# Transposing attention weights by a product with diag(1/sum), and two heads' values as the weights of one output product

## The chip, the cores and the metric

One core of a Trainium2 chip runs the whole program. The metric is the device time of one execution in microseconds (us). The engines are TensorE (PE; its weight loads are PEld), VectorE (DVE), ScalarE (ACT), GpSimd (POOL) and SyncE (SP); SP's queue issues the large loads from memory one after the other.

## The reference

A trunk of two layers over 256 context tokens and 256 latent tokens, model width 1024. Each layer has a mixer with three head groups (a state-space part S5, multi-head latent attention, an mLSTM), an output projection, and a mixture of 64 experts of which each token takes 8. All products are in fp32. Both parts are modulated by rows `mod = silu(c) @ ada_w + ada_b`. The attention has 8 heads of 64 + 32 columns for queries and keys and 64 columns for values:

```python
def _attend(q_nope, q_rope, k_nope, k_rope, v):
    s = (jnp.einsum('bqhd,bkhd->bhqk', q_nope, k_nope)
         + jnp.einsum('bqhr,bkr->bhqk', q_rope, k_rope))
    p = jax.nn.softmax(s.astype(jnp.float32) * MLA_SCALE, axis=-1).astype(v.dtype)
    return jnp.einsum('bhqk,bkhd->bqhd', p, v)
...
y_lat = jnp.concatenate([s5_lat, mla_lat, ml_lat], axis=-1) @ w_out[layer]
```

Context queries read context alone (256 keys, two blocks of 128), latent queries read context and latent (512 keys, four blocks). The second layer ("last") computes only the 256 latent queries.

## The kernel before, in words

The mixer of a layer has two stages. In the first, the input projections and S5 run; in the second, three Python generators are woven together: `mlstm`, `mla` and `more` (the modulation rows and then the loads of `w_out`). `weave` takes so many steps of each in a round: two of `mlstm`, two of `mla`, one of `more` (a step of `more` is one block of `ada_w`), in an order from the table `PACE` (`Do`); the mLSTM begins six rounds late (`latem`). What a generator issues between two `yield`s stands together in the order of each engine. So if one generator has fewer steps, the others' instructions stand at other places.

`mla` works by items, one head and one segment of queries each (`seg` 1: latent, four key blocks; `seg` 0: context, two; layer 1 has `seg` 1 alone, so 8 items; layer 0 has 16). `scores` (L907) makes two query tiles `s`, the maximum, the exponentials `pr` with their sums, and the reciprocals `sm[:, :, 2:3]`. `turn` (L924) transposes `pr` block by block with `tpose` (L312) into `pt`, key rows on the partitions. `outs` (L933) multiplies: `pt` is the stationary operand, 64 columns of the values `V` the moving one, and each result, 128 queries by 64 columns, is scaled by the reciprocal into `on` (L943 on ScalarE, L945 on VectorE). An item is in three steps of the loop at once: item n scores, n - 1 turns, n - 2 gives its output (three `yield`s an item). At the end four (layer 1: two) further steps transpose `on` (L971 to L976) into `cat`, model columns on the partitions, as the projection needs it.

`more` (L1387) runs the modulation rows: three calls of `ada_pair` in layer 0 and two in layer 1, with eight steps each. A step loads a megabyte `w` (L364) and multiplies it in four column quarters (L366). The last pair of layer 0 copies its sums `ada` on ScalarE (L371) and transposes them (`adac`, L377); the others add the bias on VectorE (L388) and write the rows to memory (L390). Behind the steps come the four megabytes of `w_out` (L353). `w` has four buffers: a load is issued when the step four before it is done. After the streams `post` projects `cat` by `w_out` (`yo`, L1430) for four token tiles (layer 1: two), normalises, and later runs the shared expert, whose weights `sw` (3 MB, L1420) are loaded to a place that the mixer's tiles used.

The order of each engine's instructions is fixed when the program is built. A scheduler puts the loads into SP's order by when their places come free; each engine and each queue then works in that order.

Of the kernel before, what the change touches and what calls it, by code (L numbers as in the profile page):

```python
# [10 lines left out]
F32 = mybir.dt.float32  # L11
BF16 = mybir.dt.bfloat16
I32 = mybir.dt.int32
AF = mybir.ActivationFunctionType
OP = mybir.AluOpType
# [256 lines left out]
class Trunk:  # L272
# [587 lines left out]
    def mla(self, l, qn, kn, kr, mp, cat, last):  # L860
        nc, d, v = self.nc, self.d, self.nc.vector
        n0 = 256 if last else 0
        wq, wkv = self.wq.rearrange("p (a b) -> p a b", a=2), self.wkv[:, :1024]
        kh = [mp.tile([96, NT], F32, name=f"kh{j}") for j in range(4)]
        for j in range(4):
            (v.tensor_copy if j % 2 else nc.scalar.copy)(kh[j][64:96], kr[64:96])
        V = mp.tile([128, 4, 512], F32, name="V")
        on = mp.tile([128, 4, 512], F32, name="on")
        qh = {}

        def values(i):
            ps = self.bank("v")
            nc.tensor.matmul(ps, kn[:, i * 128:(i + 1) * 128], wkv[:, 512:], start=True, stop=True)
            nc.scalar.copy(V[:, i, :], ps)

        def queries(h4):
            pr, pw = self.bank("qr"), self.bank("qw")
            for t, o in ((pr, 512), (pw, 768)):
                for b in range(2):
                    nc.tensor.matmul(t[:, n0:], wq[:, b, o + h4 * 128:o + h4 * 128 + 128], qn[b][:, n0:], start=b == 0, stop=b == 1)  # L880
            t1 = mp.tile([128, 256], F32, name="rp1")
            t2 = mp.tile([128, 256], F32, name="rp2")
            v.tensor_tensor(out=t1, in0=pr[:, 256:], in1=self.c("cos"), op=OP.mult)
            v.tensor_tensor(out=t2, in0=pw[:, 256:], in1=self.c("sin"), op=OP.mult)
            for j in range(4):
                h = 4 * h4 + j
                qh[h] = mp.tile([96, NT], F32, name=f"qh{j}")
                r = slice(32 * j, 32 * j + 32)
                v.tensor_tensor(out=qh[h][64:96, 256:], in0=t1[r], in1=t2[r], op=OP.add)
                if not last:  # L890
                    nc.scalar.copy(qh[h][64:96, 0:256], pr[r, 0:256])
            for p2 in range(2):
                hp = 2 * h4 + p2
                ps = self.bank("qn")
                for b in range(2):
                    nc.tensor.matmul(ps[:, n0:], wq[:, b, hp * 128:hp * 128 + 128], qn[b][:, n0:], start=b == 0, stop=b == 1)
                nc.scalar.copy(qh[2 * hp][0:64, n0:], ps[0:64, n0:])
                v.tensor_copy(qh[2 * hp + 1][0:64, n0:], ps[64:128, n0:])

        def keys(hp):  # L900
            ps = self.bank("kh")
            nc.tensor.matmul(ps, wkv[:, hp * 128:hp * 128 + 128], kn, start=True, stop=True)
            k2 = kh[2 * (hp % 2):2 * (hp % 2) + 2]
            nc.scalar.copy(k2[0][0:64], ps[0:64])
            v.tensor_copy(k2[1][0:64], ps[64:128])

        def scores(it):  # L907
            h, seg = it["h"], it["seg"]
            nk = it["nk"]
            n = nk * 128  # L910
            it["pr"] = pr = mp.tile([128, 2, NT], F32, name="pr", bufs=2)
            it["sm"] = sm = mp.tile([128, 2, 4], F32, name="sm", bufs=4)
            both = self.bank("s") if nk == 2 else None
            for t in range(2):
                qt = seg * 2 + t
                ps = both[:, t * n:(t + 1) * n] if both is not None else self.bank("s")
                nc.tensor.matmul(ps, qh[h][:, qt * 128:(qt + 1) * 128], kh[h % 4][:, :n], start=True, stop=True)
                it[t] = ps
            for t in range(2):
                v.tensor_reduce(out=sm[:, t, 0:1], in_=it[t], axis=AX.X, op=OP.max, negate=True)  # L920
                nc.scalar.activation(pr[:, t, :n], it[t], AF.Exp, bias=sm[:, t, 0:1], accum_out=sm[:, t, 1:2])
            v.reciprocal(sm[:, :, 2:3], sm[:, :, 1:2])

        def turn(it):  # L924
            nk = it["nk"]
            it["pt"] = pt = mp.tile([128, 4, 2, 128], F32, name="pt", bufs=2)
            for t in range(2):
                pp = self.bank("pt")
                for kt in range(nk):
                    self.tpose(pp[:, kt * 128:(kt + 1) * 128], it["pr"][:, t, kt * 128:(kt + 1) * 128])  # L930
                (nc.scalar.copy if t else v.tensor_copy)(pt[:, 0:nk, t], pp[:, :nk * 128].rearrange("p (k q) -> p k q", k=nk))

        def outs(it):  # L933
            h, seg, nk = it["h"], it["seg"], it["nk"]
            po = self.bank("o")
            for kt in range(nk):
                for t in range(2):
                    nc.tensor.matmul(po[:, t * 64:(t + 1) * 64], it["pt"][:, kt, t], V[:, kt, h * 64:(h + 1) * 64],
                                     start=kt == 0 and t == 0, stop=kt == nk - 1 and t == 1)
            for t in range(2):  # L940
                o, a, sc = on[:, seg * 2 + t, h * 64:(h + 1) * 64], po[:, t * 64:(t + 1) * 64], it["sm"][:, t, 2:3]
                if t:
                    nc.scalar.activation(o, a, AF.Identity, scale=sc)  # L943
                else:
                    v.tensor_scalar(out=o, in0=a, scalar1=sc, scalar2=None, op0=OP.mult)  # L945

        queries(0)
        yield
        keys(0)
        for i in range(4):  # L950
            values(i)
        yield
        items = [dict(h=h, seg=seg, nk=4 if seg else 2) for h in range(8) for seg in ((1,) if last else (1, 0))]
        for n in range(len(items) + 2):
            if n < len(items):
                h = items[n]["h"]
                if h != items[n - 1]["h"] or n == 0:
                    if h == 4:
                        queries(1)
                        yield  # L960
                    if h % 2 == 0 and h < 6:
                        keys(h // 2 + 1)
                scores(items[n])
                yield
            if 1 <= n <= len(items):
                turn(items[n - 1])
                yield
            if n >= 2:
                outs(items[n - 2])
                yield  # L970
        for qt in range(2 if last else 0, 4):  # L971
            ps = self.bank("oT")
            for b in range(4):
                self.tpose(ps[:, b * 128:(b + 1) * 128], on[:, qt, b * 128:(b + 1) * 128])
            (nc.scalar.copy if qt % 2 else v.tensor_copy)(cat[:, 0:4, qt * 128:(qt + 1) * 128], ps.rearrange("p (b n) -> p b n", b=4))
            yield  # L976


    def ml_conv(self, l, zp, w, hT, last):
# [265 lines left out]
    def mixer(self, l):  # L1245
# [131 lines left out]
        extra = late(extra, pace("late", l, 0))  # L1377
        ml = late(ml, pace("latem", l, 0))
        st = {"m": (ml, x), "a": (mla, y), "e": (extra, z)}
        weave(*(st[k] for k in pace("Do", l, "mae")))  # L1380
        self.dbg(f"cat5{l}", cat5)
# [705 lines left out]
```

## Time and profile before

| | |
|---|---|
| median of 3 executions | 1953.34 us (1949.94 to 1953.38) |
| the profiled execution | 1954.82 us, span 1953.0 us, mean granted clock 0.96 |
| TensorE busy | 1791.8 us, 92% of the span |
| VectorE, ScalarE, GpSimd busy | 776.2 (40%), 394.7 (20%), 444.5 us (23%) |
| `o`, 160 products by head (L938) | 39.5 us busy, 320 records |
| `pt`, 160 transpositions (L313) | 22.2 us busy, 160 records |

A busy time is the sum of the durations of one engine's instructions, which can overlap on TensorE; what a group costs in the engine's order is read better from the starts of it and of the next group. "Idle before" with a name in brackets is time in which the engine had nothing to do, and who released it. The granted clock is a share of TensorE's full speed. The rows themselves stand in a section below.

### The profile page before, as it was taken

The page shows a single profiled execution, that of the slowest core. Times are in us where ns is not written, and L with a number is a line of the kernel's source. Part 1 is how long each engine was busy: PE and PEld are TensorE (multiplying, and loading weights), DVE is VectorE, ACT ScalarE, POOL GpSimd, SP SyncE. Part 2 cuts the span into 40 slices and gives each one's busy share as a digit, 9 for nine tenths or more (in the row PEclk, how much of TensorE's full clock was granted, in tenths as well). Part 3 has the DMA queues.
Part 4 walks back from the last instruction along what each step waited for, and adds up shares of the span by engine and source line. Part 5 has one row for each costly group of instructions (what it writes and reads, how often), then busy time and mean ns, then how long its engine had stood idle before and what let it go on. Part 6 is the DMA issues. An engine that isn't in the chain of part 4 may idle for free. (4 is left out here: it accounts for less than half of the span.)

```text
span 1953.0 us, 29087 instructions
## 1 busy us (share of the span) xinstructions
PE 1791.8 (92%) x10161; PEld 843.2 (43%) x10161; DVE 776.2 (40%) x2258; ACT 394.7 (20%) x756; POOL 444.5 (23%) x453
## 2 busy tenths in 40 slices
PE   6999999979999999999998079899899999999993
PEld 2654665533443443334332056565444444444330
DVE  5666664852422342222221476564722222322113
ACT  2335331301111111111111233531301111011000
POOL 3120211232321332232312360002011111112312
PEclk8999999989999999999999589899999999999996
DMA  8643568299999989999998614268499999996883
GB/s 327 185 98 108 175 246 304 78 346 339 361 324 338 329 304 358 351 357 347 332 360 279 197 40 107 97 217 306 180 416 375 341 354 329 349 358 204 316 316 93
DMA packets 163329, 529.22 MB, mean 271 GB/s; under 512 B 29022, under 2 KB 46366, under 8 KB 154476
## 3 DMA queue, kind: packets, MB, share of 16 engines
q1 hardware_dynamic: 143772, 482.46, 66.8%
q0 software_dynamic: 19408, 44.87, 10.4%
q8 instruction: 82, 1.34, 0.3%
q14 instruction: 67, 0.55, 0.1%
HBM read 534.27 MB, written 49.61 MB: 299 GB/s over the span
## 5 line engine op out<-in xcount | busy, mean ns | idle before, releaser
L1823 PE MATMUL gu<-ring,xT 128*32 128x512 f32 (+3 forms) x2896 | 656.6, 601 | 8.5 <-DMA ring<-in_exp_w 8.2
L1823 PEld LDWEIGHTS gu<-ring,xT 128*32 128x32 f32 (+3 forms) x2896 | 194.4, 128 | 374.0 <-issue 315.3
L1836 PE MATMUL dn<-ring,hT 128*32 128x512 f32 (+3 forms) x1448 | 317.2, 598 | 1.8 <-DVE hT L1727 1.0
L1848 POOL DMA_INDIRECT Y<-xo,gi x79 | 120.4, 1524 | 662.4 <-DVE xo L1841 300.8
L1719 DVE TENSOR_TENSOR hh<-gu,sg 128x256 f32<-128x256 f32 (+3 forms) x86 | 36.4, 425 | 498.8 <-ACT sg L1718 498.8
L1836 PEld LDWEIGHTS dn<-ring,hT 128*32 128x32 f32 (+3 forms) x1448 | 98.6, 128 | 177.9 <-issue 158.6
L1841 DVE TENSOR_SCALAR xo<-dn,gc 128x512 f32<-128x512 f32 (+3 forms) x80 | 60.1, 751 | 228.5 <-PE dn L1836 228.5
L1718 ACT ACTIVATE sg<-gu 128x256 f32<-128x256 f32 (+3 forms) x86 | 32.8, 384 | 565.1 <-PE gu L1823 547.1
L467 PE MATMUL pT<-hT,w 128*128 128x512 f32 (+1 forms) x288 | 119.4, 568 | 2.9 <-ACT hT L458 2.9
L1848 POOL DMA_INDIRECT Y<-xo,si x66 | 90.2, 1367 | 119.5 <-DMA Y<-xo,gi 99.5
L1798 PEld LDWEIGHTS <-fb 128*128 128x128 bf16 x1536 | 86.5, 99 | 55.0 <-issue 55.0
L1840 ACT ACTIVATE xo<-dn,gc 128x512 f32<-128x512 f32 (+3 forms) x80 | 55.0, 687 | 222.3 <-PE dn L1836 219.4
L1798 PE MATMUL xT<-oneh,fb 128*128 128x128 bf16 (+4 forms) x1536 | 97.4, 220 | 0.0
L1800 ACT COPY xT<-xT 128x512 f32<-128x512 f32 (+3 forms) x80 | 45.8, 573 | 220.8 <-PE xT L1798 137.4
L1780 POOL DMA_INDIRECT xg<-fd,gi x48 | 53.4, 1112 | 135.7 <-PE xT L313 80.3
L1800 DVE COPY xT<-xT 128x512 f32<-128x512 f32 (+3 forms) x80 | 53.4, 670 | 77.3 <-PE xT L1798 43.6
L1430 PE MATMUL yo<-w,cat 128*128 128x512 f32 x192 | 83.3, 593 | 0.8 <-DMA w<-in_w_out 0.8
L467 PEld LDWEIGHTS pT<-hT,w 128*128 128x128 f32 x288 | 55.8, 198 | 55.4 <-issue 47.5
L313 PE MATMUL hT<-cst,xt 128*128 128x128 f32 x64 | 14.0, 386 | 63.1 <-ACT xt L2035 59.0
L366 PE MATMUL ada<-w,sil 128*32 128x512 f32 x384 | 56.6, 648 | 10.5 <-DMA w<-in_ada_w 10.5
L475 PE MATMUL pN<-w,hT 128*128 128x256 f32 (+2 forms) x256 | 61.0, 395 | 0.0
L313 PEld LDWEIGHTS xT<-cst,xg 128*128 128x128 f32 (+4 forms) x384 | 41.1, 140 | 38.8 <-issue 36.0
(567 smaller groups left out, 2038.7 us busy)
## 6 DMA issues: line engine op xcount, KB each, us to landing
ring<-in_exp_w SPq DMA_DIRECT2D x768, 512.0 KB
w<-in_ada_w SPq DMA_DIRECT2D x48, 1024.0 KB
w<-in_w_out SPq DMA_DIRECT2D x8, 1024.0 KB
Y<-zeros SPq DMA_DIRECT2D x12, 512.0 KB
sw<-in_sh_w SPq DMA_DIRECT2D x2, 3072.0 KB
w<-in_w_uv SPq DMA_DIRECT2D x4, 1024.0 KB
w<-in_w_mm SPq DMA_DIRECT2D x4, 1024.0 KB
w<-in_w_qk SPq DMA_DIRECT2D x4, 768.0 KB
```

The lines of the kernel that those rows point to most:

```text
L313: self.nc.tensor.transpose(out, in_, self.c("ident")[:in_.shape[0], :in_.shape[0]])
L366: nc.tensor.matmul(ps[32 * q:32 * q + 32, :], self.sil[:, k, :], t[:, q * 512:(q + 1) * 512], start=k == 0, stop=k == 7, tile_position=(0, ...
L467: self.nc.tensor.matmul(ps[base:base + m, n0:NT], w[k][:, col:col + m], hT[:, k, n0:NT], start=k == 0, stop=k == 7)
L475: self.nc.tensor.matmul(ps[:, :n], hT[:, k, i * 128:(i + 1) * 128], w[k][:, col:col + n], start=k == 0, stop=k == 7)
L1430: nc.tensor.matmul(st[at][n], cb[:, i * 128:(i + 1) * 128], wo[n][b], start=b == 0, stop=b == 7)
L1798: nc.tensor.matmul(o, self.fb[i][:, z, cs], t["oh"][:, i, 0:m], start=at == 0, stop=at + 1 == len(parts))
L1800: (nc.scalar.copy if hh else v.tensor_copy)(o, a)
L1823: nc.tensor.matmul(t["gu"][r, :], t["xt"][:, 2 * c + b, r], ws[j][:, b * 512:(b + 1) * 512], start=c == 0 and b == 0, stop=c == 3 and b == ...
L1836: nc.tensor.matmul(po[n][r, :], t["ht"][:, b, r], ws[b * nr + j][:, n * 512:(n + 1) * 512], start=b == 0, stop=b == 1, **kw)
L1840: nc.scalar.activation(xo[0:m, 0:512], po[0][0:m], AF.Identity, scale=t["gc"][0:m])
L1841: v.tensor_scalar(out=xo[0:m, 512:1024], in0=po[1][0:m], scalar1=t["gc"][0:m], scalar2=None, op0=OP.mult)
L1848: nc.gpsimd.indirect_dma_start(out=y, out_offset=bass.IndirectOffsetOnAxis(ap=si[0:cap], axis=0), in_=xo[col:col + cap], in_offset=None, c ...
```

## The change

`scores` makes one more tile per item, `dg`: for each query tile the identity, with its rows multiplied by the reciprocal of the sums (one instruction on VectorE, one on ScalarE). `turn` no longer transposes: it is a plain product with the block of `pr` as the stationary operand and `dg` as the moving one, which gives the transposed and divided weights; `pt` has four buffers instead of two. `outs` works once per pair of heads. `V` is the stationary operand, 64 columns of each head, and `pt` with 256 query columns the moving one; the two heads go to the two halves of the array's columns (`tile_position`), so the result has the two heads' columns on 128 partitions, as `cat` needs them, and is copied there at once. The tile `on`, the scalings and the last transpositions are gone. The items come pairwise, both heads of a pair for one segment, and `mla` has 2.5 steps an item in place of 3, and none behind the loop.

```diff
--- before.py
+++ after.py
@@ -865,7 +865,6 @@
         for j in range(4):
             (v.tensor_copy if j % 2 else nc.scalar.copy)(kh[j][64:96], kr[64:96])
         V = mp.tile([128, 4, 512], F32, name="V")
-        on = mp.tile([128, 4, 512], F32, name="on")
         qh = {}
 
         def values(i):
@@ -920,29 +919,33 @@
                 v.tensor_reduce(out=sm[:, t, 0:1], in_=it[t], axis=AX.X, op=OP.max, negate=True)
                 nc.scalar.activation(pr[:, t, :n], it[t], AF.Exp, bias=sm[:, t, 0:1], accum_out=sm[:, t, 1:2])
             v.reciprocal(sm[:, :, 2:3], sm[:, :, 1:2])
+            it["dg"] = dg = mp.tile([128, 2, 128], F32, name="dg", bufs=3)
+            for t in range(2):
+                if t:
+                    nc.scalar.activation(dg[:, t], self.c("ident"), AF.Identity, scale=sm[:, t, 2:3])
+                else:
+                    v.tensor_scalar(out=dg[:, t], in0=self.c("ident"), scalar1=sm[:, t, 2:3], scalar2=None, op0=OP.mult)
 
         def turn(it):
             nk = it["nk"]
-            it["pt"] = pt = mp.tile([128, 4, 2, 128], F32, name="pt", bufs=2)
+            it["pt"] = pt = mp.tile([128, 4, 2, 128], F32, name="pt", bufs=4)
             for t in range(2):
                 pp = self.bank("pt")
                 for kt in range(nk):
-                    self.tpose(pp[:, kt * 128:(kt + 1) * 128], it["pr"][:, t, kt * 128:(kt + 1) * 128])
+
+                    nc.tensor.matmul(pp[:, kt * 128:(kt + 1) * 128], it["pr"][:, t, kt * 128:(kt + 1) * 128], it["dg"][:, t], start=True, stop=True)
                 (nc.scalar.copy if t else v.tensor_copy)(pt[:, 0:nk, t], pp[:, :nk * 128].rearrange("p (k q) -> p k q", k=nk))
 
         def outs(it):
-            h, seg, nk = it["h"], it["seg"], it["nk"]
+
+            seg, nk, hp = it["seg"], it["nk"], it["h"] // 2
             po = self.bank("o")
             for kt in range(nk):
-                for t in range(2):
-                    nc.tensor.matmul(po[:, t * 64:(t + 1) * 64], it["pt"][:, kt, t], V[:, kt, h * 64:(h + 1) * 64],
-                                     start=kt == 0 and t == 0, stop=kt == nk - 1 and t == 1)
-            for t in range(2):
-                o, a, sc = on[:, seg * 2 + t, h * 64:(h + 1) * 64], po[:, t * 64:(t + 1) * 64], it["sm"][:, t, 2:3]
-                if t:
-                    nc.scalar.activation(o, a, AF.Identity, scale=sc)
-                else:
-                    v.tensor_scalar(out=o, in0=a, scalar1=sc, scalar2=None, op0=OP.mult)
+                for x in (it["mate"], it):
+                    o = slice(64 * x["o"], 64 * x["o"] + 64)
+                    nc.tensor.matmul(po[o, 0:256], V[:, kt, x["h"] * 64:(x["h"] + 1) * 64], x["pt"][:, kt].rearrange("p t q -> p (t q)"),
+                                     start=kt == 0, stop=kt == nk - 1, tile_position=(0, o.start))
+            (nc.scalar.copy if hp % 2 else v.tensor_copy)(cat[:, hp, seg * 256:(seg + 1) * 256], po[:, 0:256])
 
         queries(0)
         yield
@@ -950,30 +953,26 @@
         for i in range(4):
             values(i)
         yield
-        items = [dict(h=h, seg=seg, nk=4 if seg else 2) for h in range(8) for seg in ((1,) if last else (1, 0))]
+        items = [dict(h=2 * hp + o, o=o, seg=seg, nk=4 if seg else 2) for hp in range(4) for seg in ((1,) if last else (1, 0)) for o in range(2)]
+        for a, b in zip(items[::2], items[1::2]):
+            b["mate"] = a
         for n in range(len(items) + 2):
             if n < len(items):
                 h = items[n]["h"]
-                if h != items[n - 1]["h"] or n == 0:
+                if h % 2 == 0 and items[n]["seg"]:
                     if h == 4:
                         queries(1)
                         yield
-                    if h % 2 == 0 and h < 6:
+                    if h < 6:
                         keys(h // 2 + 1)
                 scores(items[n])
                 yield
             if 1 <= n <= len(items):
                 turn(items[n - 1])
                 yield
-            if n >= 2:
+            if n >= 2 and items[n - 2]["o"]:
                 outs(items[n - 2])
                 yield
-        for qt in range(2 if last else 0, 4):
-            ps = self.bank("oT")
-            for b in range(4):
-                self.tpose(ps[:, b * 128:(b + 1) * 128], on[:, qt, b * 128:(b + 1) * 128])
-            (nc.scalar.copy if qt % 2 else v.tensor_copy)(cat[:, 0:4, qt * 128:(qt + 1) * 128], ps.rearrange("p (b n) -> p b n", b=4))
-            yield
 
 
     def ml_conv(self, l, zp, w, hT, last):
```

Three places of the order follow, from the program before and from the changed one. TensorE, the end of layer 0's second mixer stage, before: `o` and `oT` are the attention's output and its transposition, `hT` the mLSTM's output transposed, `ada` steps of the modulation, four products each.

```order
L366 MATMUL ada<-w,sil 32x512 x4
L313 MATMUL pt<-cst,pr 128x128 x8
L938 MATMUL o<-V,pt 128x64 x4
L366 MATMUL ada<-w,sil 32x512 x4
L313 MATMUL pt<-cst,pr 128x128 x4
L938 MATMUL o<-V,pt 128x64 x8
L366 MATMUL ada<-w,sil 32x512 x4
L938 MATMUL o<-V,pt 128x64 x4
L313 MATMUL oT<-cst,on 128x128 x12
L377 MATMUL adac<-cst,adarow 128x8 x4
L313 MATMUL oT<-cst,on 128x128 x4
L1430 MATMUL yo<-w,cat_110 128x512 x2
```

The same place in the changed program:

```order
L916 MATMUL s<-kh_1357,qh_1929 128x256 x2
L936 MATMUL pt<-dg,pr 128x128 x4
L313 MATMUL hT_2449<-cst,hs 128x128 x2
L366 MATMUL ada<-w,sil 32x512 x4
L946 MATMUL o<-pt,V 64x256 x8
L936 MATMUL pt<-dg,pr 128x128 x4
L366 MATMUL ada<-w,sil 32x512 x4
L946 MATMUL o<-pt,V 64x256 x4
L366 MATMUL ada<-w,sil 32x512 x16
L377 MATMUL adac<-cst,adarow 128x8 x4
L1429 MATMUL yo<-w,cat_110 128x512 x2
```

The attention's last output stands four steps of `ada` ahead of `adac`, and no transposition is left beside them.

SP, the end of layer 1's second mixer stage, before: `w` are blocks of `ada_w` or `w_out`, `modd_71` the modulation rows in memory, `sw` the shared expert's weights.

```order
L364 DMA w<-in_ada_w 128x2048 x3
L353 DMA w<-in_w_out 128x2048 x2
L390 DMA modd_71<-adarow 2x512 x4
L353 DMA w<-in_w_out 128x2048 x2
L395 DMA g_9963<-modd_71 128x1024
L1404 DMA pxt<-x2d 128x1024 x2
L1414 DMA ln1g<-in_lnp 128x1024
L1415 DMA ln1b<-in_lnp 128x1024
L395 DMA sc_9971<-modd_71 128x1024
L395 DMA sh_9973<-modd_71 128x1024
L1419 DMA rw<-in_router_w 128x512
L1420 DMA sw<-in_sh_w 128x6144
```

The same place in the changed program:

```order
L364 DMA w<-in_ada_w 128x2048 x2
L1419 DMA sw<-in_sh_w 128x6144
L364 DMA w<-in_ada_w 128x2048 x2
L353 DMA w<-in_w_out 128x2048 x2
L390 DMA modd_71<-adarow 2x512 x4
L353 DMA w<-in_w_out 128x2048 x2
L395 DMA g_9869<-modd_71 128x1024
```

The load of `sw` has moved ahead of the last two blocks of `ada_w` and of all of `w_out`.

TensorE, the end of layer 1's second mixer stage, before: `num` and `int` are parts of the mLSTM's output.

```order
L938 MATMUL o<-V,pt 128x64 x8
L313 MATMUL oT<-cst,on 128x128 x3
L366 MATMUL ada<-w,sil 32x512
L313 MATMUL oT<-cst,on 128x128
L366 MATMUL ada<-w,sil 32x512 x4
L313 MATMUL hT_9901<-cst,hs 128x128 x2
L313 MATMUL oT<-cst,on 128x128 x4
L366 MATMUL ada<-w,sil 32x512 x11
L1430 MATMUL yo<-w,cat_8132 128x512 x2
```

The same place in the changed program:

```order
L946 MATMUL o<-pt,V 64x256 x8
L366 MATMUL ada<-w,sil 32x512 x4
L1151 MATMUL num<-va,E 128x65 x4
L1161 MATMUL int<-C_9454,mqk_8774 128x65
L1161 MATMUL int<-C_9454,mqk_8775 128x65
L1161 MATMUL int<-C_9454,mqk_8774 128x65
L1161 MATMUL int<-C_9454,mqk_8775 128x65
L366 MATMUL ada<-w,sil 32x512 x4
L313 MATMUL hT_9786<-cst,hs 128x128 x2
L366 MATMUL ada<-w,sil 32x512 x8
L313 MATMUL hT_9813<-cst,hs 128x128 x2
L366 MATMUL ada<-w,sil 32x512 x8
```

The last `o` stands ahead of the last `num` and `int`, and six steps of `ada` follow it, in place of four.

## Rows read from the trace of the kernel before

**Rows 1.** Windows, both attention stretches: us, PE, PEld, DVE, ACT, POOL, clock, DMA, GB/s.

```profile
182.00:303.70 121.70, 120.44 (x863) 78.60 (x862) 74.56 (x232) 48.05 (x128) 20.32 (x29) 1.00 0.62 215
1262.00:1337.50 75.50, 74.85 (x543) 48.36 (x545) 46.89 (x137) 27.81 (x67) 10.94 (x18) 1.00 0.57 200
```

**Rows 2.** Groups by line and form, TensorE: products by head, transpositions of the weights.

```profile
L938 PE MATMUL o<-V,pt 128*128 128x64 f32 x320 | 39.5, 274 | 0.0
L313 PE MATMUL pt<-cst,pr 128*128 128x128 f32 x160 | 22.2, 277 | 0.0
```

**Rows 3.** Timeline of TensorE, layer 1: start, us, line, xrecords, [idle before].

```profile
1289.59 0.69 PE L1109 MATMUL st<-va,ek 128*64 128x65 f32 x16
1290.20 1.12 PE L902 MATMUL kh<-kn,w 128*128 128x512 f32 x2
...
1300.72 1.95 PE L1134 MATMUL mb<-AM,cst 64*128 64x128 f32 x16
1302.60 1.09 PE L313 MATMUL pt<-cst,pr 128*128 128x128 f32 x8
1303.53 1.90 PE L938 MATMUL o<-V,pt 128*128 128x64 f32 x16
...
1326.22 0.67 PE L1162 MATMUL int<-C,mqk 64*128 64x65 f32 x8
...
1335.95 0.44 PE L313 MATMUL hT<-cst,hs 128*128 128x128 f32 x2 [0.65 <-POOL hs L1195]
...
1340.32 4.99 PE L1430 MATMUL yo<-w,cat 128*128 128x512 f32 x11 [0.79 <-DMA w<-in_w_out]
```

**Rows 4.** Timeline of TensorE, end of layer 0's mixer.

```profile
282.50 0.44 PE L313 MATMUL hT<-cst,hs 128*128 128x128 f32 x2 [0.81 <-POOL hs L1195]
...
296.76 0.66 PE L313 MATMUL pt<-cst,pr 128*128 128x128 f32 x4
297.25 1.90 PE L938 MATMUL o<-V,pt 128*128 128x64 f32 x16
299.08 1.06 PE L366 MATMUL ada<-w,sil 128*32 128x512 f32 x8
300.08 1.10 PE L938 MATMUL o<-V,pt 128*128 128x64 f32 x8
301.02 1.65 PE L313 MATMUL oT<-cst,on 128*128 128x128 f32 x12
302.51 0.96 PE L377 MATMUL adac<-cst,adarow 128*128 128x8 f32 x8
...
303.79 8.75 PE L1430 MATMUL yo<-w,cat 128*128 128x512 f32 x20
```

**Rows 5.** Timeline of TensorE, an expert whose second product runs in two halves.

```profile
522.13 3.65 PE L1836 MATMUL dn<-ring,hT 128*64 128x512 f32 x16
525.72 0.65 PE L313 MATMUL hT<-cst,hh 128*128 128x128 f32 x4
```

**Rows 6.** Groups by line, VectorE: a 128x128 block scaled and shifted.

```profile
L460 DVE TENSOR_SCALAR hT<-hT,modc 128x128 f32<-128x128 f32 x32 | 11.7, 406 | 6.2 <-ACT hT L458 6.2
```

**Rows 7.** Timeline of ScalarE, end of layer 0's mixer.

```profile
300.21 0.59 ACT L371 COPY adarow<-ada 128x512 f32<-128x512 f32 x1 [0.39 <-PE ada L366]
```

**Rows 8.** Timeline of SP, which issues the large loads, end of layer 1's mixer.

```profile
1335.35 2.84 SPq L353 DMA_DIRECT2D w<-in_w_out  x2
...
1350.92 0.33 SPq L1420 DMA_DIRECT2D sw<-in_sh_w  x1
```

**Rows 9.** Timeline of TensorE, start of the kernel.

```profile
24.82 1.94 PE L366 MATMUL ada<-w,sil 128*32 128x512 f32 x8 [1.42 <-DMA w<-in_ada_w]
...
27.30 1.94 PE L366 MATMUL ada<-w,sil 128*32 128x512 f32 x8 [0.54 <-DMA w<-in_ada_w]
```

**Rows 10.** Windows of 2 us, start of the kernel, columns as in the first group.

```profile
26.00:28.00 2.00, 1.46 (x8) 0.20 (x8) 0.00 (x0) 0.00 (x0) 0.00 (x0) 0.50 1.00 418
...
38.00:40.00 2.00, 2.00 (x4) 0.95 (x3) 2.00 (x8) 1.16 (x3) 1.92 (x3) 0.50 1.03 373
```

## The prediction

> **What bounds the kernel now.** I read the share of each engine first, then the two stretches in which the attention runs. The page gives TensorE 92% of the span, and the two stretches, the second half of the mixer of each layer, are fuller still: 120.44 of 121.70 us and 74.85 of 75.50 us, at a granted clock of 1.00, while VectorE has 61 to 62%, ScalarE 37 to 40% and the DMA engines 57 to 62% [rows 1]. So inside these stretches TensorE's own content is the time, and work of VectorE and ScalarE counts only where TensorE has nothing else to do. That is at their ends, where the projection `yo` has to wait for the last product of a woven stream. So I then read TensorE's order of time over both ends [rows 3, 4], and the queue of SP beside the second one [rows 8].
>
> **TensorE's content.** Costs are taken from the start of one group to the start of the next. An fp32 product leaves two records, a transposition one: 160 products `o` by head are 320 records, 160 transpositions are 160 [rows 2] (layer 0 has 8 items of eight blocks and 8 of four, layer 1 has 8 of eight). Eight transpositions cost 1303.53 − 1302.60 = 0.93 us [rows 3], four 297.25 − 296.76 = 0.49 [rows 4]. A plain fp32 product of 128 moving columns has a near row in `mb`: 16 records 1302.60 − 1300.72 = 1.88 [rows 3]. So a turn by `dg` costs 1.88 for eight blocks and 1.0 for four. That is 8 × 0.95 + 8 × 0.5 = 11.6 more in layer 0, and 8 × 0.95 = 7.6 more in layer 1.
>
> The old `o` costs 299.08 − 297.25 = 1.83 per item of 16 records and 301.02 − 300.08 = 0.94 per item of 8 [rows 4]. The new one takes two heads at once: eight products of 256 columns, four in each column half. Halves do run side by side in this kernel: 16 records of 512 columns in two halves take 525.72 − 522.13 = 3.59 [rows 5], that is 0.43 for each pair in which one alone would last as long. With 256 columns a pair of records is 0.213: 8 × 0.213 + 0.15 = 1.85 per pair of heads with four key blocks, and 1.0 with two. Layer 0: 8 × 1.83 + 8 × 0.94 = 22.2 becomes 4 × 1.85 + 4 × 1.0 = 11.4, so −10.8. Layer 1: 14.6 becomes 7.4, so −7.2. The 0.15 for the change to halves is from `st`, whose 16 records of 65 columns cost 1290.20 − 1289.59 = 0.61, where 8 pairs of 0.054 would be 0.43 [rows 3].
>
> The 24 transpositions of `on` go: 16 in layer 0 (302.51 − 301.02 = 1.49 for twelve [rows 4], four more by that 0.5) and eight in layer 1 (1.0). Layer 0 comes to +11.6 − 10.8 − 2.0 = −1.2, layer 1 to +7.6 − 7.2 − 1.0 = −0.6. TensorE thus does about 2 us less in all; the swap itself is close to even.
>
> The Trainium skill, "Perfetto Trace Analysis", Transposes, speaks against the change: a logical transposition should be one, and not a standard product, since transpositions skip the arithmetic. By that rule alone the edit would be a loss, the 19.2 of the turns. The rows agree on the direction and the size (two records for one), but show 21 taken away by what the product makes possible; the sum goes by them.
>
> **VectorE and ScalarE.** Per item one `dg` on each is added (nearest row 406 ns, a 128x128 block on VectorE [rows 6]); one scaling of 128x64 on each and the six copies of `oT` go, and twelve copies of 128x256 come. With 38 to 40% of their time free beside a full TensorE I take 0; bounds −1 and +2. The wait this adds, a turn behind `dg` behind the reciprocal, has an item's step between; TensorE has `ada` and mLSTM work in that place. It is bare only at the ends.
>
> **The end of layer 0.** The mLSTM's last `hT` waited 0.81 for GpSimd [rows 4]; that place is now a turn which waits for `dg`, with the norm's VectorE work in front of it: I take 1.2, so +0.4. Attention now has 2.5 steps per item where it had 3, so it ends before the `ada` stream: four whole steps (16 products) and `adac` stand behind the last `o`, where now twelve transpositions stood between the last step and `adac`. A step is 300.08 − 299.08 = 1.0 [rows 4]; the last one's megabyte can be asked for only when its buffer is free, at the end of the step four before it. A lone megabyte takes 1340.32 − 1335.35 = 5.0 from its issue to its first use [rows 3, 8]; between lie the last `o` (1.0) and three steps (3.1), so it is 0.9 late. `adac` then waits for ScalarE's copy of the sums, 0.59 long [rows 7], formerly under `oT`: 0.8. Sum: −1.2 + 0.4 + 0.9 + 0.8 = +0.9, say **+1** (bounds −2, if all of it is hidden, and +4).
>
> **The end of layer 1.** Here the order of SP's queue changes. The shared expert's 3 MB `sw` stands now behind everything, issued at 1350.92 [rows 8], since its place in the on-chip memory is that of `V`, `on` and queries, read until the last `oT`. Without `on` the tiles lie otherwise: its place is that of `V`, `pr`, `dg`, free after the last `o`; and the queue has `sw` ahead of the last two `ada` loads and all four of `w_out`. When is that? Before, the last `int` group ends at 1326.89 [rows 3]. Now all eight turns and all four `o` stand ahead of it, where seven turns and six `o` stood: 8 × 1.88 − 7 × 0.93 + 4 × 1.85 − 6 × 1.83 = +4.9, so 1331.8. The last `o` is 2.6 before (a step of `ada`, `num`, `int`): 1329.2. `sw` is issued 0.3 later. With the queue full, one megabyte's step follows the other after 2.5 (24.82 to 27.30 for two steps, the DMA engines at 1.00 and 418 GB/s [rows 9, 10]). First megabyte of `sw` 1334.5, third 1339.5, the two `ada` loads 1342.0 and 1344.5, the first of `w_out` **1347.0**. `yo` started at 1340.32 [rows 3]: **+6.7**. The mLSTM's last `hT`, 9.1 behind the last `int` as before (1335.95 − 1326.89), comes at 1340.9 and is covered. From there `yo` needs 3.5 us per megabyte of `w_out` (8 records of 0.43, 303.79 on: 20 in 8.75 [rows 4]), so the next loads keep up, and the delay stays until the end. Nothing comes back: `sw` is read after both tiles' projections, norms and transpositions.
>
> While TensorE waits there it has 1 us steps between gaps of 1.5. At the kernel's start such a stretch shows the granted clock at 0.50, the 1.2 GHz level, and it is still 0.50 in a stretch in which TensorE is busy throughout, 2.00 of 2.00 us [rows 10]. If `yo` begins at that level for 4 us it loses 2; I take **+1.5** (0 to 2).
>
> **Sum.** +1 + 6.7 + 1.5 = +9.2 on the profiled execution's 1954.82 us (span 1953.0). That execution is 1.5 above the median of the runs, 1953.34, so the forecast is 1953.34 + 9.2 = **1962.5**. Its own range is 1957.5 (the tail of layer 1 half as late) to 1967 (both ends at their upper bounds).
>
> **Rivals.** *A: the transfers do not queue behind `sw`.* If the later megabytes share the engines with it, or the queue has the space sooner, `yo` of layer 1 starts only with TensorE's own order, at about 1341.5: +1.2, and with layer 0's +1 some +2: 1955.5. For it: the DMA engines are only 57% busy in that stretch [rows 1]. Against: at the kernel's start the loads land in the order of their issue, 2.5 apart. *B: the other side.* Only TensorE's content counts: `w_out` is there before the last step ends, the clock stays at 1.00, and the tails shed what they held, −1.8 of content and the 0.79 for which `yo` waited for `w_out` [rows 3]: −2.6, 1950.7. It decides if `sw` is issued later than its place in the queue lets me think, or the first of `w_out` lands before TensorE has done its last step. Against it stands the queue's order. *C: the two halves do not run side by side with V as weights.* Forty pairs of key blocks (24 and 16) times 0.43 more: +17, 1979. Against it: the rows of `dn` and `st`. *D: a transposition is much cheaper than a plain product beyond what the records show.* By the rows it is half, two records against one. If it were a quarter, the turns would cost 3 × 0.116 × 160 = +56 instead of +19, and the time were 2000; the row of `mb` speaks against it.
>
> The Trainium skill, "TensorE: Matmul & The Clock Gate", Terms, gives a transposition mode four times faster for fp32. The rows here bear out a factor of two; D is what the page's factor would make.
>
> **Chances.** Forecast 0.63, A 0.22, B 0.10, C 0.03, D 0.02. The range of 8 in 10 goes from 1951, which takes in A and most of B's edge, to 1969. About 0.2% (3.9 us) is what a measurement of this kernel can tell from no change: 1949.4 to 1957.2. Of the forecast nine tenths lie above it, of A a tenth, and C and D wholly: slower 0.64. Of B some six tenths are faster: 0.07 with what the forecast's far edge adds. The rest, 0.29, is the same.
>
> **What would show it.** In the changed kernel's trace: 320 records of `pt` of about 0.117 each from start to start; `o` groups of 1.85; in SP's queue the issue of `sw` near 1329; in TensorE's order at the end of layer 1 steps of `ada` with waits for the DMA of 1.5 and more in front, and `yo` near 1347 plus what layer 0 adds; a granted clock below 1.00 at its start. If `yo` waits for no DMA there, the forecast is wrong in its largest term; if turns or `o` differ from 1.88 and 1.85, in the content.

## The result, and the profile after

The changed kernel takes 1973.68 us (median of 4 executions, 1971.31 to 1974.2), the one before 1953.36: a ratio of 1.0108 with a 95% interval of 1.0095 to 1.0121. It is slower, as forecast, but by 20.3 us where 9.2 were forecast, and beyond the range's upper end of 1969. Its profiled execution took 1974.19, with a span of 1972.0, 19.0 more than the span before.

Where the 19.0 arise is read from the start of the same instruction in both traces:

| landmark on TensorE | before | after | late by |
|---|---|---|---|
| first `qr` of layer 0's attention | 174.1 | 173.9 | −0.2 |
| first `yo`, layer 0 | 303.8 | 309.2 | 5.4 |
| first `fT`, layer 0 (behind the first 96 records of `yo`) | 345.0 | 353.0 | 8.0 |
| last `yT`, layer 1's first stage | 1238.9 | 1246.5 | 7.5 |
| first `yo`, layer 1 | 1340.3 | 1355.8 | 15.5 |
| last `yo`, layer 1 | 1367.5 | 1384.4 | 16.9 |
| last `lg`, layer 1 | 1388.0 | 1407.6 | 19.5 |
| last `gu` of the experts | 1907.4 | 1926.7 | 19.3 |

So 8 us arise at the end of layer 0's attention, 8 at the end of layer 1's, and 4 in the projection and the normalisation behind that. One caution for all such sums: between `fT` of layer 0 and the last `yT`, where all the kernels do the same work, the eleven traces take from 888.0 to 894.0 us, so a landmark behind it carries several us of chance. Stages are therefore compared from `yT` on.

TensorE's content came out nearly as worked out. The groups by line and form in the trace after, answering to [rows 2]:

```profile
L936 PE MATMUL pt<-dg,pr 128*128 128x128 f32 x320 | 41.3, 280 | 2.0 <-DVE dg L927 2.0
L946 PE MATMUL o<-pt,V 128*64 128x256 f32 x160 | 20.8, 399 | 0.0
```

Twice the records for the turns, half the records for `o`. What a group costs stands in the timeline of TensorE at the end of layer 1, answering to [rows 3]:

```profile
1328.79 1.95 PE L946 MATMUL o<-pt,V 128*64 128x256 f32 x16
1330.67 2.05 PE L936 MATMUL pt<-dg,pr 128*128 128x128 f32 x16
1332.65 1.07 PE L366 MATMUL ada<-w,sil 128*32 128x512 f32 x8
...
1335.28 1.95 PE L946 MATMUL o<-pt,V 128*64 128x256 f32 x16
1337.16 1.07 PE L366 MATMUL ada<-w,sil 128*32 128x512 f32 x8
...
1347.52 0.44 PE L313 MATMUL hT<-cst,hs 128*128 128x128 f32 x2 [4.44 <-POOL hs L1194]
1349.87 1.94 PE L366 MATMUL ada<-w,sil 128*32 128x512 f32 x8 [1.91 <-DMA w<-in_ada_w]
1353.37 1.93 PE L366 MATMUL ada<-w,sil 128*32 128x512 f32 x8 [1.57 <-DMA w<-in_ada_w]
1355.80 24.44 PE L1429 MATMUL yo<-w,cat 128*128 128x512 f32 x53 [0.49 <-DMA w<-in_w_out]
```

`o` costs 1330.67 − 1328.79 = 1.88 (1.85 forecast), a turn 1.98 (1.88 forecast). The lower rows are the mechanism forecast for this place: the last two steps of `ada`, and then `yo`, wait for their loads. (`hT` waits 4.44 for GpSimd first; the load behind it comes later still.) SP's timeline, answering to [rows 8], has the reason, `sw` issued 0.15 after the last `o` gives way to the next group (1337.16) and ahead of all of them:

```profile
1337.31 0.33 SPq L1419 DMA_DIRECT2D sw<-in_sh_w  x1
1338.29 2.96 SPq L364 DMA_DIRECT2D w<-in_ada_w  x2
1342.28 1.19 SPq L353 DMA_DIRECT2D w<-in_w_out  x2
```

The end of layer 0 is the place that was mis-sized. TensorE's timeline there, answering to [rows 4]:

```profile
289.23 1.13 PE L916 MATMUL s<-kh,qh 96*128 96x256 f32 x4
292.35 1.13 PE L936 MATMUL pt<-dg,pr 128*128 128x128 f32 x8 [2.00 <-DVE dg L927]
293.32 0.38 PE L313 MATMUL hT<-cst,hs 128*128 128x128 f32 x2
293.63 1.85 PE L366 MATMUL ada<-w,sil 128*32 128x512 f32 x8
295.41 2.81 PE L946 MATMUL o<-pt,V 128*64 128x256 f32 x16
298.15 1.16 PE L936 MATMUL pt<-dg,pr 128*128 128x128 f32 x8
...
305.26 1.07 PE L366 MATMUL ada<-w,sil 128*32 128x512 f32 x8 [1.23 <-DMA w<-in_ada_w]
307.03 1.54 PE L377 MATMUL adac<-cst,adarow 128*128 128x8 f32 x8 [0.70 <-ACT adarow L371]
309.18 43.96 PE L1429 MATMUL yo<-w,cat 128*128 128x512 f32 x96 [0.61 <-DMA w<-in_w_out]
```

There are four waits, 2.00, 1.23, 0.70 and 0.61, and slow work behind them: the step of `ada` at 293.63 lasts 1.85, elsewhere 1.07, the `o` at 295.41 lasts 2.81 in place of 1.95, `adac` 1.54 in place of 0.96 [rows 4]. The windows of the same trace show why (columns as in [rows 1]; the granted clock is the number behind the last bracket):

```profile
294.00:297.00 3.00, 3.00 (x16) 0.99 (x10) 0.45 (x2) 1.03 (x4) 0.00 (x0) 0.50 0.27 35
304.00:309.00 5.00, 2.63 (x20) 1.60 (x16) 0.38 (x4) 0.58 (x1) 0.00 (x0) 0.84 1.01 410
309.00:315.00 6.00, 5.82 (x8) 2.57 (x9) 0.00 (x0) 0.00 (x0) 0.00 (x0) 0.56 1.00 415
307.50:314.20 6.70, 6.09 (x12) 3.16 (x12) 0.38 (x4) 0.00 (x0) 0.00 (x0) 0.50 1.02 429
```

After each of the two idle stretches the clock was granted at 0.50, the 1.2 GHz level, and it was back at 1.00 later; the means 0.84 and 0.56 are of windows that hold both levels. The first stretch costs 0.8 in `ada` and 0.9 in `o`, the second 0.6 in `adac` and 2.6 in `yo`, whose 96 records take 43.96 where the trace before has this row:

```profile
303.79 41.37 PE L1430 MATMUL yo<-w,cat 128*128 128x512 f32 x96
```

The four waits (4.5) and the low clock (4.8), less the 1.3 for which TensorE waited in this stage before (0.81 of it in [rows 4]) and 0.2 of an earlier start, are 7.9 of the 8.0. The content of the stage, summed from the start of each group to the next without waits and low clock, is the same in both traces (128.5). The first wait is made on VectorE; its timeline:

```profile
290.26 0.16 DVE L921 RECIPROCAL sm<-sm 128x2 f32<-128x2 f32 x1
291.58 0.43 DVE L1088 TENSOR_TENSOR hs<-hs,hrs 128x256 f32<-128x256 f32 x1 [1.16 <-POOL hrs L1190]
291.92 0.28 DVE L927 TENSOR_SCALAR dg<-cst,sm 128x128 f32<-128x128 f32 x1
```

The reciprocal is there at 290.42. `dg` stands in VectorE's order behind a step of the mLSTM's norm, which waits 1.16 for GpSimd, and TensorE waits for `dg`.

### The profile page after: what moved, and what is told of

Read it like the earlier page. It is cut to its first block, busy times and chain, and to the rows that moved or that the text cites. A ratio compares the mean times of both kernels' runs of the same rounds, so it can differ in the third digit from the quotient of the medians.

```text
span 1972.0 us, 29059 instructions
## 1 busy us (share of the span) xinstructions
PE 1799.3 (91%) x10137; PEld 841.0 (43%) x10137; DVE 777.8 (39%) x2261; ACT 397.3 (20%) x759; POOL 445.8 (23%) x453
## 5 line engine op out<-in xcount | busy, mean ns | idle before, releaser
L1429 PE MATMUL yo<-w,cat 128*128 128x512 f32 x192 | 87.3, 616 | 1.1 <-DMA w<-in_w_out 1.1
L1429 PEld LDWEIGHTS yo<-w,cat 128*128 128x128 f32 x192 | 37.8, 199 | 49.2 <-issue 48.5
```

The lines of the kernel that those rows point to most:

```text
L1429: nc.tensor.matmul(st[at][n], cb[:, i * 128:(i + 1) * 128], wo[n][b], start=b == 0, stop=b == 7)
```

## The experiments

The theory: the loss stands at the two ends, where TensorE waits, for loads above all, and at a low clock afterwards; the arithmetic is about even. The rival: the arithmetic is the loss, since a plain fp32 product costs more than a transposition, and the ends only show it.

**`sw` behind `w_out`.** One small copy makes the load wait:

```diff
+        nc.gpsimd.tensor_copy(sw[:, 0, 0:1], wo[1][7][:, 0:1])
         nc.sync.dma_start(sw, d["sh_w"][l].rearrange("p (c f) -> p c f", c=6))
```

> The changed kernel (1973.7 us), with one small GpSimd copy that makes the load of sw wait for the last megabyte of w_out; in layer 1 it then stands behind all of them in SP's queue, layer 0 keeps its order. Theory (the loss stands at the two ends of the attention, the place of sw being the largest single part): yo of layer 1 starts about 6 us earlier against layer 0's landmarks, and the idle stretch before the second tile's fT (3.63 us, with the low clock behind it, 2.7 in all) goes too: -8.7, about 1965. Rival (the dearer product of the turn is the loss, the ends are only where it shows): no change, 1973.7.

Measured: 1965.3, ratio to before 1.0054 (1.0036 to 1.0072), 8.4 less than the changed kernel. In TensorE's timeline `yo` of layer 1 now starts with no wait for a load:

```profile
1343.97 0.44 PE L313 MATMUL hT<-cst,hs 128*128 128x128 f32 x2 [3.10 <-POOL hs L1194]
1344.34 3.46 PE L366 MATMUL ada<-w,sil 128*32 128x512 f32 x14
1347.72 28.15 PE L1430 MATMUL yo<-w,cat 128*128 128x512 f32 x64
```

By the medians the place of `sw` is worth 8 us. The trace shows some 5 of them in their place: from the last `yT` to `yo` it takes 104.8, where the changed kernel takes 109.3 and the one before 101.4, and `yo` is 1.0 shorter. The rest of the 8 lies elsewhere in the execution. The 3.4 that this stage still loses are mostly `hT`, which now waits 3.10 for GpSimd where it waited 0.65 [rows 3]: behind the loads this wait was hidden. The idle time before the second `fT` did not go as expected (2.78 in place of 3.63).

**`dg` on ScalarE alone.**

```diff
             for t in range(2):
-                if t:
-                    nc.scalar.activation(dg[:, t], self.c("ident"), AF.Identity, scale=sm[:, t, 2:3])
-                else:
-                    v.tensor_scalar(out=dg[:, t], in0=self.c("ident"), scalar1=sm[:, t, 2:3], scalar2=None, op0=OP.mult)
+                nc.scalar.activation(dg[:, t], self.c("ident"), AF.Identity, scale=sm[:, t, 2:3])
```

> The changed kernel with both halves of dg made by ScalarE, so that none stands behind the mLSTM's norm on VectorE. Theory: at layer 0's end the 2.00 us wait for dg shrinks to about 1.0 and the stretch at granted clock 0.50 behind it (1.7 lost) goes or shortens: -1 to -2.7, 1971 to 1972.7. Rival (ScalarE becomes the bound inside the stretch, since it gets 24 more instructions of 0.4): slower by up to 5. Rival of content: no change.

Measured: 1974.31, ratio 1.0105 (1.0086 to 1.0123): no gain. In the trace the wait did shrink, and `yo` of layer 0 starts 2.4 earlier, 0.5 of it from an earlier start of the attention:

```profile
290.58 1.16 PE L933 MATMUL pt<-dg,pr 128*128 128x128 f32 x8 [0.57 <-ACT dg L924]
292.54 0.44 PE L313 MATMUL hT<-cst,hs 128*128 128x128 f32 x2 [0.80 <-POOL hs L1191]
...
302.92 1.06 PE L366 MATMUL ada<-w,sil 128*32 128x512 f32 x8 [1.26 <-DMA w<-in_ada_w]
```

Part of the time went to `hT`, which needs the same norm and now waits for it itself; the wait for the load stayed. The lead is still 2.7 at layer 1's first `yo`, 1.2 at the last `lg` and 0.5 at the last `gu` of the experts. Whether the edit is worth 1 or 2 us lies below what these executions tell; what took the lead back is open.

**The old count of steps.** The attention gives way to the other streams as often as before:

```diff
-            if n >= 2 and items[n - 2]["o"]:
-                outs(items[n - 2])
+            if n >= 2:
+                if items[n - 2]["o"]:
+                    outs(items[n - 2])
                 yield
+        for _ in range(2 if last else 4):
+            yield
```

> The changed kernel with the attention's old count of steps: a yield also after the items that give no output, and four (layer 1: two) behind the loop. The arithmetic is the changed one, the ada steps stand again between the last turns, and sw is again last in SP's queue. Theory: waits for the last ada loads and the low clock at both ends go; what stays is content (-2) and up to 2 of a wait for dg: 1951 to 1957. Rival (the dearer turn is the loss): 1970 or more.

Measured: 1956.1, ratio 1.0016 (1.0005 to 1.0027). This edit alone, with the arithmetic of the change untouched, takes back 17.6 of the 20.3 us. Its timeline at the end of layer 0 has no wait left for `dg`, a load or `adarow`; the mLSTM's `hT` waits for GpSimd, 1.65 in place of 0.81. `yo` starts within 0.2 of its old place:

```profile
284.74 0.44 PE L313 MATMUL hT<-cst,hs 128*128 128x128 f32 x2 [1.65 <-POOL hs L1197]
...
302.04 1.08 PE L946 MATMUL o<-pt,V 128*64 128x256 f32 x8
303.05 1.06 PE L377 MATMUL adac<-cst,adarow 128*128 128x8 f32 x8
303.96 16.55 PE L1432 MATMUL yo<-w,cat 128*128 128x512 f32 x38
...
1333.90 0.44 PE L313 MATMUL hT<-cst,hs 128*128 128x128 f32 x2 [1.95 <-POOL hs L1197]
...
1338.68 11.73 PE L1432 MATMUL yo<-w,cat 128*128 128x512 f32 x26
```

In layer 1 `yo` starts 1.6 earlier than before, but that lead stems from the stretch between the layers (at the last `yT` it is 3.2): from the last `yT` to `yo` the stage takes 102.9, 1.5 longer than before, with `hT` waiting 1.95 in place of 0.65. No load is waited for, and `sw` is last in its queue, since the last `o` comes later. The rival is refuted: with all the dearer turns in it the kernel is within 0.3% of the one before.

**The three together.**

> The three edits together: old count of steps, dg on ScalarE alone, sw behind w_out. Theory: as the one with the steps alone, less the rest of the wait for dg: 1950 to 1955. Rival (the dearer turn is the loss): 1970 or more.

Measured: 1954.95, ratio 1.0005 (0.9996 to 1.0015): level with the kernel before.

**The old count of steps in layer 0 alone**, by making the two additions above only where the layer isn't the last.

> The changed kernel with the old count of steps in layer 0 alone; layer 1 keeps the change's order with sw ahead of the last ada loads. Theory: layer 0's part of the loss (8.0 by the landmarks at the first fT) goes, layer 1's 12 stays: 1965 to 1967. Rival (the part of layer 0 is hidden later, as the gain at its end was when dg went to ScalarE): 1971 to 1974.

Measured: 1963.67, ratio 1.0057 (1.0039 to 1.0074): 10.0 less than the changed kernel, a little below the range expected. Up to the first `fT` its trace takes back 7.9, all that layer 0 had lost. Together with the 8.4 of `sw`, the 10.0 come to the 17.6 of the old steps in both layers within their intervals: two losses that add up.

**`dg` alone on the kernel before.** Output by head, `on` and `oT` stay; the scaling becomes a copy, and `dg` is made as in the changed kernel.

```diff
-                    self.tpose(pp[:, kt * 128:(kt + 1) * 128], it["pr"][:, t, kt * 128:(kt + 1) * 128])
+                    nc.tensor.matmul(pp[:, kt * 128:(kt + 1) * 128], it["pr"][:, t, kt * 128:(kt + 1) * 128], it["dg"][:, t], start=True, stop=True)
```

> The kernel before with one part of the change alone: dg and the turn by a plain product; output by head, on, its copies (without scaling), oT and the steps as before, sw last in SP's queue. Theory: content alone, two records for one: +19 of turns, 1972, with no new waits for the last ada loads. Rival (a plain product costs four times a transposition): +56, 2009.

Measured: 1972.27, ratio 1.0097 (1.008 to 1.0113), 20.1 more than its own runs of before. From start to start its turns take 37.6 in both layers, where they took 18.9. The price of the plain product is two for one; four for one is refuted.

**The other part alone: transpositions, output by pairs.** Steps and `sw` mended, `dg` gone, `tpose` back in the turn. The division of the weights by their sums is left out.

> The changed kernel with the old count of steps and sw behind w_out, and the turns as transpositions again, without dg: the weights are not divided by their sums (that part of the computation is left out). Theory: TensorE's content is the time inside the stretches, so the turns' 19.2 us come off the 1955 to 1956 of the kernel with the product: 1937. Rival (TensorE's time there is hidden behind VectorE's and ScalarE's chains once the ends are mended): 1950 or more.

Measured: 1938.62, ratio 0.9926 (0.9904 to 0.9948): 16.3 less than the three together with `dg`, where 19.2 were forecast.

**The same with the division ahead of the transposition:**

```diff
             v.reciprocal(sm[:, :, 2:3], sm[:, :, 1:2])
+            for t in range(2):
+                if t:
+                    nc.scalar.activation(pr[:, t, :n], pr[:, t, :n], AF.Identity, scale=sm[:, t, 2:3])
+                else:
+                    v.tensor_scalar(out=pr[:, t, :n], in0=pr[:, t, :n], scalar1=sm[:, t, 2:3], scalar2=None, op0=OP.mult)
```

> As the one before, but the weights are divided before they are transposed, by one instruction per query tile on VectorE or ScalarE over the whole row of weights (256 or 512 columns) in place of dg; it computes the whole reference. Theory: VectorE and ScalarE have 38 to 63% of their time free in the stretches, so the time stays near the kernel without the division: 1937 to 1942, faster than both kernels by 0.6 to 0.8%. Rival (the longer chain from the exponentials to the turn leaves TensorE waiting, an item's step is not enough): 1948 to 1955.

Measured: 1940.21, ratio 0.9929 (0.9912 to 0.9946): 12.0 faster than the kernel before and 33 faster than the changed one. Two groups and one window of its trace:

```profile
L313 PE MATMUL pt<-cst,pr 128*128 128x128 f32 x160 | 22.1, 277 | 0.0
L945 PE MATMUL o<-pt,V 128*64 128x256 f32 x160 | 20.5, 386 | 0.0
```

```profile
182.00:297.00 115.00, 113.23 (x752) 62.99 (x751) 77.45 (x235) 54.42 (x133) 19.96 (x30) 1.00 0.62 215
```

TensorE keeps the cheap turns and the cheap `o`, and VectorE and ScalarE, 67% and 47% busy in this stretch, hide nearly all of the division: it costs 1.6 by the medians, less than the spread of either kernel's executions.

**Filling the waits.** The changed kernel with 25 transpositions of a constant at the end of layer 0, to keep TensorE busy in three of its four waits there; the order of the rest is untouched.

```diff
+        end = l == 1 and g == 0
+        fb = self.bank("fill") if end else None
+        def fill(n):
+            for _ in range(n if end else 0):
+                self.tpose(fb[:, 0:128], self.c("ident"))
...
+            if k == 7:
+                fill(11)
...
+            fill(7)
             ps = self.bank("adac")
...
+            fill(7)
```

> The changed kernel with 25 extra transpositions of a constant, which nobody reads, at the end of layer 0's attention: 11 ahead of the last ada step, where TensorE waits 1.23 us for its megabyte, 7 ahead of adac (0.70) and 7 ahead of yo (0.61). The order of the loads and the waits stay. Theory (the waits themselves are 2.5 us, and the granted clock falls to 0.50 because TensorE stands idle in them, which costs another 3 in adac and the first 7 us of yo): with TensorE busy the clock stays at 1.00 over 304 to 315 and the first fT comes 2 to 3 us earlier, 1971; adac and yo take 41.4 in place of 43.96 for their first 96 records. Rival (the low clock is not from the idle time, or the 96 records wait for w_out): the granted clock falls as before, the time is the same or up to 1 us more, 1974.

Measured: 1968.6, ratio 1.0083 (1.0064 to 1.0102); by the medians 5 less than the changed kernel, though the intervals overlap. The trace is plainer:

```profile
303.87 1.42 PE L313 MATMUL fill<-cst 128*128 128x128 f32 x11
305.22 1.06 PE L373 MATMUL ada<-w,sil 128*32 128x512 f32 x8
306.21 0.98 PE L313 MATMUL fill<-cst 128*128 128x128 f32 x7
307.03 1.01 PE L385 MATMUL adac<-cst,adarow 128*128 128x8 f32 x8
307.90 0.96 PE L313 MATMUL fill<-cst 128*128 128x128 f32 x7
309.19 41.47 PE L1438 MATMUL yo<-w,cat 128*128 128x512 f32 x96 [0.32 <-DMA w<-in_w_out]
```

```profile
304.00:309.00 5.00, 4.86 (x41) 3.59 (x41) 0.39 (x4) 0.59 (x1) 0.00 (x0) 1.00 1.00 388
309.00:315.00 6.00, 5.81 (x14) 2.71 (x15) 0.00 (x0) 0.00 (x0) 0.00 (x0) 1.00 1.02 423
```

`yo` starts at the same time, but at full clock, and its 96 records take 41.47 where they took 43.96. The waits for these loads are there without the fillers in two more traces, of the kernels with `sw` behind `w_out` and with `dg` on ScalarE: the clock fell in both, and the 96 records took 43.13. With fillers there is one trace. So the low clock came from the idle time and not from the loads, as far as one trace with fillers can show it.

## Why the prediction was wrong

Step by step:

- *TensorE's content, −2 in all.* Right to within 1. `o` 1.88 for 1.85 (the row of `st` gives 0.61 − 0.43 = 0.18 for the change to halves, not 0.15), turns 1.79 to 1.98 for 1.88, halves side by side. Summed from start to start over both stretches, the turns cost 19.6 more, `o` 17.4 less at full clock, the transpositions of `on` 3.2 less: −1.0. In layer 0 all groups together come to 0 where −1.2 was in the sum. The two parts alone bear it out: +20.1 for the turns, and with transpositions and the mended ends −13.6 against the kernel before, where −21 of content was worked out. In the trace with transpositions the work of the two stretches is 10.8 and 6.5 less from start to start, 17.3 of the 21, and 1.5 of the rest is low clock at the end of layer 1. Behind the projection 3 more were lost, as told below.
- *The rule against the change.* The Trainium skill, "Perfetto Trace Analysis", Transposes, holds here in its direction: keeping the transposition and dividing ahead of it is worth 15 us against the product with `dg` at nearly equal ends (1940.21 and 1954.95).
- *The end of layer 0, "+1 (bounds −2, and +4)".* This is the step that failed: it measured 8.0 in the trace, and 10.0 by the run that undoes it. The waits came where they were forecast: `dg` 2.00 for 1.2, the load 1.23 for 0.9, `adac` 0.70 for 0.8, and 0.61 for `w_out`, which had none. What had no place in the sum is the clock. The prediction priced it in layer 1 and gave layer 0 none, though the same kind of waits were forecast there. It cost 4.8 in this execution, the largest single miss; the content, −1.2 in the sum and 0 in the trace, is the next. The 4.8 are partly chance: with the same order in layer 0, the kernel with `sw` behind `w_out` shows only the second fall in its trace, and loses 1.9.
- *The end of layer 1, +6.7.* Right: 15.47 − 7.54 = 7.9 in the trace. The run that puts `sw` behind takes 8.4 off the whole, but 4.5 off this stage, since `hT`, which the prediction had as covered, then waits in the open. `sw` was forecast 0.3 behind the last `o` and came 0.15 behind it; the loads queue behind it, 3.5 and 2.4 from one step to the next. Rival A, that they don't, is refuted.
- *The clock in layer 1, +1.5.* Right in size: `yo` is 16.9 − 15.5 = 1.4 longer, and begins at the low clock:

```profile
1356.00:1359.00 3.00, 3.00 (x4) 1.25 (x5) 0.12 (x1) 0.00 (x0) 0.00 (x0) 0.54 0.30 76
```

- *"The delay stays until the end."* Wrong by 2.6. Behind the projection TensorE waits for the second tile's normalisation, 3.63 in one piece, and the clock falls once more, where nothing hides it (`fT` starts as long after the last `yo` as before, and from there to the last `lg` it takes 7.7 in place of 5.0):

```profile
1396.00:1400.00 4.00, 0.37 (x2) 0.17 (x2) 3.45 (x8) 1.00 (x4) 1.61 (x2) 0.96 0.56 188
1400.00:1406.00 6.00, 6.00 (x21) 4.64 (x22) 3.05 (x3) 2.49 (x3) 0.00 (x0) 0.50 0.11 42
```

The trace before has the low clock earlier in this place, in products of `gu` that end before that normalisation does, so it delayed nothing:

```profile
1372.00:1376.00 4.00, 3.86 (x11) 2.47 (x12) 3.34 (x17) 2.62 (x4) 0.74 (x2) 0.58 0.02 4
```

In the kernel with the old steps it fell late too (`fT` behind 2.77 of idle time), though `sw` was last there; with all three edits `fT` waited 1.0. So these 2.6 are not a matter of `sw` alone; what decides them is not shown.

In sum, about 9 of the 19.0 are low clock (4.8, 1.4 and 2.6), of which the prediction had 1.5.

## What to carry to other kernels

A change of arithmetic also changes how often a stream gives way to others, and with that who is last: here the swap with the old count of steps cost some 3 us (1956.1 for 1952.77), and the count of steps 18. Read the order at the ends first, and look which load moves ahead when a tile's life gets shorter. Then price each forecast wait of TensorE twice, once as the wait and once for the work that follows it at half clock; and look whether half of a change, here the pairs without the product by `dg`, is better than the whole.

## What the runs showed of the hardware

The same wait does not always lower the clock. TensorE waited 2.00 us for `dg` in the changed kernel and 2.01 in the one with fillers, with the same instructions around it. In the first the following three us had a granted clock of 0.50 (window 294 to 297 above), in the second of 1.00:

```profile
294.00:297.00 3.00, 3.00 (x26) 1.78 (x28) 1.30 (x5) 2.08 (x7) 0.37 (x1) 1.00 0.40 167
```

The kernel with `sw` behind `w_out` has the wait of 2.00 too, and behind it `ada` and `o` take 1.06 and 1.95, as at full clock. So such a wait may cost 1.6 more in one execution than in another, and the second group of waits cost 1.9 in that kernel where it cost 3.2 in the changed one. The 19 runs of before that stood beside the first four experiments go from 1949.67 to 1958.57; whether several such falls make up that spread is not shown. Transpositions of a constant were enough to hold the clock at 1.00 in the one trace that has them.
